# Softmax sums and turned maxima share one PSUM bank behind the V products; a maximum over partitions by matmul; two small re-orderings

## The chip, the core and the metric

The kernel runs on one core of a Trainium2 chip. That core has five engines with a queue each: TensorE (PE; its weight loads are listed as PEld), VectorE (DVE), ScalarE (ACT), GpSimd (POOL) and SyncE (SP, which here only issues DMAs). The metric is device time in microseconds (us); lower is better. Before the change it is 2773.54 us, the median of three runs (2772.81 to 2776.64).

## The reference: what is computed

One bidirectional encoder layer is applied to two requests of 2048 tokens and 1024 features with the same weights:

```python
u = rmsnorm(h);  q, k, v, ga, f, gf = split(u @ w_in)     # 512,128,128,512,512,512 columns
q, k = rope(rmsnorm(q)), rope(rmsnorm(k))                 # 8 query heads, 2 key/value heads of 64
a  = softmax(q k^T / 8) v * silu(ga)
fo = Re(fft2 over positions and 64 channels of f) @ w_fmix * silu(gf)
h  = h + concat(a, fo) @ w_out
h  = h + (p @ w_ple) * sigmoid(rmsnorm(h) @ w_ple_gate)
y  = rmsnorm(h)
```

All data are float32 and large gains make the softmax sharp, so the kernel splits the matrix operands into a high and a low half-precision part (three products for each matmul) and subtracts the exact row maximum ahead of the exponential.

## The kernel before, in words

**Stages.** Three stages follow one another. From 0 to about 845 us the projections (line L444) run and their results go to DRAM. From there to about 2697 us attention runs, and while it runs a second stream of work, the *filler*, is cut into its steps: first the Fourier branch (`fourier2`, L1010 to L1072), then the output projection, the gate and the norms (`outp`, L1445). What is left of the filler when attention ends is the *tail*.

**Attention.** A unit `u` is a block of 128 queries of one request and one key/value head with four query heads; there are `n` = 64 units with eight steps `j` = 0 to 7 each, one for every 256 keys. A step `g = 8u + j` issues, in this order: deferred work (`flush`), the scores of step j (`scores`, L1137, then two exponentials on ACT, L1140, and an addition of the exponentials on POOL, L1143/L1145), one eighth of the row maxima of a later unit (`maxima`: two matmuls at L1164 into the tile `ps_m`, one reduction on DVE at L1172), and at j = 4 and j = 0 the products of four steps with V (`pv`, L1202). A step with such products is called heavy. `ps_m` has one buffer, so the maxima matmuls of a step can begin only when DVE has done the reduction of the step before.

**Row sums.** At j = 4 of unit u, ahead of the products with V, `sums(u-1)` multiplies the added exponentials by ones (L1236) into a bank, and DVE takes the reciprocal (L1238) and scales the result (L1239).

**Turned maxima.** At j = 4 ACT writes the negated maxima of unit u+1 to `nm` (L1182); at j = 6 `max_rows(u+1)` turns them with an identity matmul (L1188) into another bank, and DVE writes `mr` from it (L1190). The first scores of unit u+1 read `mr`.

**The banks.** Both take a PSUM bank from `bank()`. In the first part of the filler that is one of three (`ps_f`, `ps_g` twice); once `outp` has begun (`self.grouped`) it is always the single buffer `ps_f`, which the filler's embedding product (L444, `ps_f<-wp,pT`, released by DVE at L1405 and L1407) uses too.

**Order and pace.** During attention PE, ACT, DVE and SP run in the order in which the program is written (`manual_schedule`); POOL is ordered by a planner with a cost model. `interleave` hands the filler a budget after each step, `FILL` = 775 us of the program's own accounting in all; a heavy step yields a share of 0, so nothing is normally filled in behind it. In the tail the planner orders all engines.

**The scale of the output projection.** `mix(s)` needs a maximum over 128 partitions of three per-partition maxima: `mix_max` reduces on DVE and calls `partition_all_reduce` on POOL (L1310), `mix_scale` works on the result (L1316 and after). It runs twice, once for each request.

**Loads and stores touched.** `fourier2` loads `bd` (L1734, 512 KB, in `fill`) and `c2x` (L1037) ahead of the first `c` (L979) and `g_in` (L984), all on SP. `project` collects the stores of transposed q and k in `stores_next` (L739, L743) and issues them at the start of the next iteration:

```python
            stores, stores_next = stores_next, []
            for f in stores:
                f()
            ...
            if i == n + 3:
                self.drain(bg)
                self.drain(self.ahead)
                for f in stores_next:
                    f()
```

`lo_q(i - 3)`, which fills that list, runs for the last time in iteration n + 2. The DRAM store of a unit's result (`agd<-at`, L1242) is issued on SP in the step after `sums`. In `slot`, a small copy `seen` (L1422) on DVE makes the second half of a grouped projection wait for the first.

Of the kernel before, what the change touches and what calls it, by code (L numbers as in the profile page):

```python
# [10 lines left out]
F32 = mybir.dt.float32  # L11
# [3 lines left out]
ALU = mybir.AluOpType  # L15
AX = mybir.AxisListType
PSUM = bass.MemoryType.PSUM
# [10 lines left out]
K_ONE = 2.0 ** 12  # L28

CAP = 5.0  # L30
FILL = 775.0
AHEAD = 13
PVG = 4
NBF = 5
# [10 lines left out]
_E = mybir.EngineType  # L45
# [94 lines left out]
class Build:  # L140
    def __init__(self, ctx, tc, a, y):
        self.ctx, self.tc, self.nc = ctx, tc, tc.nc
        self.a, self.y = a, y
        nc = self.nc
        ep = ctx.enter_context
        self.const = ep(tc.tile_pool(name="const", bufs=1))
        self.st = ep(tc.tile_pool(name="st", bufs=2))
        self.psF = ep(tc.tile_pool(name="psF", bufs=1, space=PSUM))
        self.psG = ep(tc.tile_pool(name="psG", bufs=2, space=PSUM))
        self.grouped = False  # L150
# [408 lines left out]
    def project(self, P, PU, W, early, wkv, wq, wga, bg, mid):  # L559
# [3 lines left out]
        nc, st = self.nc, self.st  # L563
# [159 lines left out]
        def lo_q(i):  # L723
            s, c = steps[i]
            t1 = T1.pop(i)
            qs, ks = QS.pop(i)
            res = KD.pop(i)
            kv = lambda b: ks[:, :, b].rearrange("p v t d -> p t v d")
            KS[i] = P.tile([128, CH, 2, 64], F32, name="ksum", bufs=1)
            nc.vector.tensor_tensor(out=res[:], in0=res[:], in1=kv(1), op=ALU.subtract)  # L730
            nc.vector.tensor_copy(kv(2), res[:])
            nc.vector.tensor_tensor(out=res[:], in0=res[:], in1=kv(2), op=ALU.subtract)
            nc.vector.tensor_tensor(out=KS[i][:], in0=t1[:, :, 8:10, :], in1=res[:], op=ALU.subtract)
            nc.vector.tensor_tensor(out=qs[:, :, :, 1, :], in0=t1[:, :, 0:8, :], in1=qs[:, :, :, 0, :], op=ALU.subtract)
            for tt in range(CH):
                t = c * CH + tt
                qT = P.tile([128, 8, 128], F16, name="qT", bufs=2)
                nc.sync.dma_start_transpose(qT[:], qs[:, tt].rearrange("p h b d -> p (h b d)"))
                stores_next.append(lambda t=t, qT=qT: nc.sync.dma_start(self.qTd[s][t], qT[:]))  # L739
            kT = P.tile([128, 2, 3, 128], F16, name="kT", bufs=1)  # L740
            nc.sync.dma_start_transpose(kT[:].rearrange("p v y r -> p (v y) r"),
                                        ks[:].rearrange("p v y t d -> p (v y t d)"))
            stores_next.append(lambda: nc.sync.dma_start(self.kTd[s][:, :, c].rearrange("v p y r -> p v y r"), kT[:]))  # L743

        def sweep_part(us):

# [31 lines left out]
        def iteration(i):  # L778
# [180 lines left out]
    def fourier2(self, pool, hook):  # L959
# [135 lines left out]
    def attention(self, kvp):  # L1095
# [89 lines left out]
        def max_rows(u):  # L1185

            ps = self.bank()
            nc.tensor.matmul(ps[:, 0:128], nm[:], self.ident[:], start=True, stop=True)  # L1188
            MR[u] = mr = kvp.tile([128, 4, 128], F16, name="mr", bufs=1)
            nc.vector.tensor_tensor(out=mr[:], in0=ps[:, 0:128].unsqueeze(1).to_broadcast([128, 4, 128]),  # L1190
                                    in1=own[:].unsqueeze(2).to_broadcast([128, 4, 128]), op=ALU.mult)

        def pv(u, j0):
# [32 lines left out]

            self.defer(lambda: self.defer(add))

        def sums(u):

            s, kv, t = units[u]
            acc, at = ACC.pop(u), AT.pop(u)
            av = acc[:, 0, :].rearrange("p (c e q) -> p e c q", e=2, q=128)
            ps = self.bank()
            for e in range(2):
                nc.tensor.matmul(ps[64 * e:64 * e + 64, 0:256], ones[:], av[:, e], start=True, stop=True)  # L1236
            r, x = ps[:, 256:512], at[:].rearrange("p c q -> p (c q)")
            nc.vector.reciprocal(r, ps[:, 0:256])  # L1238
            nc.vector.tensor_tensor(out=x, in0=x, in1=r, op=ALU.mult)  # L1239
# [23 lines left out]
            if k == 1 and 0 <= v - 1 < n:  # L1263
                negate(v - 1)

        def turn(g):
            v, k = divmod(g + 2, 8)
            if k == 0 and 0 <= v < n:
                max_rows(v)
# [9 lines left out]
        ones = pool.tile([128, 64], F32, name="ones", bufs=1)  # L1279
        nc.gpsimd.memset(ones[:], 1.0)  # L1280
        fresh = {last[0, kv]: kv for kv in range(2)}
        for g in range(8 * n + 7):
            self.step = g
            self.flush()
            u, j = g // 8, g % 8
            if j == 0 and 0 <= u and u + 2 < n:
                load_q(u + 2)
            if j == 4 and u - 1 in fresh:
                load_kv(1, fresh[u - 1])
            if 0 <= u < n:  # L1290
                scores(u, j)
            self.drain(lead(g))
# [6 lines left out]
            turn(g)  # L1299
            yield 0 if heavy else RATE if g >= 8 * n // 2 else 1 if g > FIRST else SLOW  # L1300


    def mix_max(self, s):
        nc, st = self.nc, self.st
        m = st.tile([128, 4], F32, name="mx4")
# [4 lines left out]
        nc.gpsimd.partition_all_reduce(mm[:, 0:3], m[:, 0:3], 128, bass_isa.ReduceOp.max)  # L1310
        return mm

    def mix_scale(self, s, mm):
        nc, st = self.nc, self.st
# [7 lines left out]

    def mix(self, s, out):

        sc = []
        yield from self.after(self.defer(lambda: sc.append(self.mix_max(s))), 1)
        yield from self.after(self.defer(lambda: out.append(self.mix_scale(s, sc[0]))))

    def outp(self, pool0, ow, open_pool):

# [305 lines left out]
    def run(self):  # L1636
# [91 lines left out]

        def fill():
            self.nw2k = NW  # L1730
            C0 = fill_stack.enter_context(pool("C0", side="right"))
            with pool("B", side="right") as B:
                self.bd = B.tile([128, 2, 4, 128], F32, name="bd")
                nc.sync.dma_start(self.bd[:], self.bdd)  # L1734
                ow = {}

                def wload(n, k, pool):
# [90 lines left out]
```

## Time and profile before

| | |
|---|---|
| median of three runs | 2773.54 us |
| the profiled execution: its own time | 2775.26 us |
| its span (first to last instruction) | 2773.5 us |
| mean granted TensorE clock | 0.989 |
| busy share PE / DVE / ACT / POOL | 96 / 61 / 44 / 59 % |
| DMA, mean over the span | 107 GB/s |

The profile comes from one execution whose own time is 1.72 us above the median and 1.76 us above its span. A group line names the source line, engine, operation and tiles, then the count, the busy time and the mean duration in ns, and last the idle time ahead of it and what ended that. In a timeline a row gives start, length, engine and line; square brackets hold the idle time of that engine just before. "issue" means that the engine was idle with no visible cause. Ends of matmuls are modelled, so two rows on PE overlap a little; starts are the better measure.

### The profile page before, as it was taken

Reading aid. Unit: us, or ns where it says so; the run is one execution under the profiler, and the core shown is the slowest. Engines: PE = TensorE matmul, PEld = TensorE weight load, DVE = VectorE, ACT = ScalarE, POOL = GpSimd, SP = SyncE. Lnnn points to the kernel's source line nnn. Section 1 sums busy time; section 2 is a strip of 40 time slices with the busy share of each in tenths; the row PEclk is TensorE's granted clock in tenths of the full one; section 3 lists DMA queues with packets and bytes.
Section 4 is the critical chain, followed back from the end, with each engine's and each line's share of the span. In section 5 each row is a group of like instructions: output and inputs, shape, how many; then the busy total and the mean of one; then the engine's idle time right before and its main releaser. Section 6 shows DMA issues by size and latency. Waiting matters only on the chain.

```text
span 2773.5 us, 46318 instructions
## 1 busy us (share of the span) xinstructions
PE 2656.9 (96%) x18236; PEld 1264.5 (46%) x18236; DVE 1684.4 (61%) x2469; ACT 1214.7 (44%) x2047; POOL 1636.9 (59%) x1394
## 2 busy tenths in 40 slices
PE   6899999999998989999999999999999999999998
PEld 3455565655555543443444434433443344434433
DVE  6755555564564664666666766666656666666644
ACT  3443333432224543554445554444444445444541
POOL 1233224332336786777768877776677677767760
PEclk9999999999999999999999999999999999999998
DMA  7467566674428752222222223322222232222222
GB/s 231 143 192 187 175 184 180 185 179 121 129 70 238 236 169 88 56 71 54 69 56 54 69 67 82 82 62 71 56 67 60 60 82 54 67 71 64 63 73 61
DMA packets 418555, 296.74 MB, mean 107 GB/s; under 512 B 259456, under 2 KB 360000, under 8 KB 418336
## 3 DMA queue, kind: packets, MB, share of 16 engines
q1 hardware_dynamic: 405424, 252.01, 34.7%
q0 software_dynamic: 12912, 41.77, 4.2%
q8 instruction: 143, 2.34, 0.3%
q14 instruction: 76, 0.62, 0.1%
HBM read 149.50 MB, written 86.51 MB: 85 GB/s over the span
## 4 chain that ended last, share of the span: by engine, by line
PE 83%; DVE 7%; issue 3%; DMA 2%; POOL 2%; ACT 2%; SPq 0%; DVEq 0%; POOLq 0%; ACTq 0%
PE ps_g L1445 22%; PE ps_o L1202 15%; PE ps_x L444 14%; PE ps_s L1137 12%; PE ps_f L444 6%; PE ps_g L444 6%; PE ps_m L1164 3%; DVE a_mx L1172 1%; PE ps_f L1236 1%; PE ps_f L1188 1%; ACT p L1140 1%; POOL acc L1145 1%; PE ps_g L1056 1%; DVE h L1407 1%; DVE ps_f L1405 1%
## 5 line engine op out<-in xcount | busy, mean ns | idle before, releaser
L1145 POOL TENSOR_TENSOR acc<-acc,p 128x1024 f32<-128x1024 f32 x384 | 917.2, 2388 | 225.4 <-ACT p L1140 163.2
L1140 ACT ACTIVATE p<-ps_s,s_scale 128x512 f32<-128x512 f32 x1024 | 648.0, 684 | 692.9 <-PE ps_s L1137 667.4
L1172 DVE TENSOR_REDUCE a_mx<-ps_m 128x1 f32<-128x1024 f32 x499 | 610.4, 1223 | 534.6 <-PE ps_m L1164 525.6
L1445 PE MATMUL ps_g<-w_pg,hT 64*128 64x512 f16 x2832 | 507.8, 378 | 5.4 <-DVE seen L1422 3.0
L1202 PE MATMUL ps_o<-p,v 128*64 128x512 f32 x2048 | 467.0, 598 | 0.0
L1137 PE MATMUL ps_s<-q,k 64*128 64x512 f16 x3072 | 438.7, 378 | 7.6 <-ACT p L1140 7.4
L444 PEld LDWEIGHTS <-uc 128*128 128x128 f16 x3072 | 301.6, 98 | 311.3 <-issue 22.1
L1445 PEld LDWEIGHTS <-hT 64*128 64x128 f16 x2832 | 206.2, 94 | 169.4 <-issue 19.7
L1445 PE MATMUL ps_g<-w_wo,mh 64*128 64x512 f16 x1488 | 269.6, 378 | 3.6 <-DVE mh L1367 2.3
L1137 PEld LDWEIGHTS <-k 64*128 64x128 f16 x3072 | 148.8, 94 | 261.2 <-issue 140.5
L1445 PE MATMUL ps_g<-w_wo,mT 64*128 64x512 f16 x1488 | 264.5, 376 | 0.4 <-DMA mT<-mh 0.3
L1202 PEld LDWEIGHTS ps_o<-p,v 128*64 128x64 f32 x2048 | 143.8, 137 | 255.7 <-issue 247.2
L1164 PE MATMUL ps_m<-k,q 64*128 64x512 f16 x998 | 205.1, 377 | 16.6 <-DVE a_mx L1172 15.7
L1143 POOL TENSOR_TENSOR acc<-p,p 128x1024 f32<-128x1024 f32 x64 | 150.5, 2352 | 98.2 <-ACT p L1140 97.9
L444 PEld LDWEIGHTS <-w_ga 128*128 128x128 f16 x1536 | 151.5, 99 | 53.1 <-issue 22.6
L926 POOL DMA_DIRECT2D gfd<-gt x32 | 19.3, 602 | 218.1 <-DVE gt L954 213.2
L1445 PEld LDWEIGHTS <-mh 64*128 64x128 f16 x1488 | 101.7, 94 | 97.9 <-issue 17.4
L1445 PEld LDWEIGHTS <-mT 64*128 64x128 f16 x1488 | 107.2, 94 | 81.2 <-DMA mT<-mh 1.3
L1218 ACT ACTIVATE tb<-ps_o,a_scale 64x256 f32<-64x256 f32 x128 | 60.1, 469 | 164.2 <-PE ps_o L1202 163.4
L444 PE MATMUL ps_x<-uc,w_ga 128*128 128x256 f16 x1008 | 115.0, 275 | 5.1 <-ACT ge L911 4.5
L944 POOL DMA_DIRECT2D agd<-gat x64 | 35.9, 561 | 134.1 <-DVE gat L954 134.0
L1238 DVE RECIPROCAL ps_f<-ps_f 128x256 f32<-128x256 f32 x60 | 105.4, 1756 | 7.6 <-PE ps_f L1236 7.6
(317 smaller groups left out, 3365.7 us busy)
## 6 DMA issues: line engine op xcount, KB each, us to landing
q<-qTd SPq DMA_DIRECT2D x256, 64.0 KB, 2.3
ag<-agd SPq DMA_DIRECT2D x64, 256.0 KB, 3.2
out<-h POOLq DMA_DIRECT2D x31, 512.0 KB, 3.2
x<-in_x_prompt SPq DMA_DIRECT2D x16, 512.0 KB, 4.8
w_st<-in_w_out SPq DMA_DIRECT2D x32, 256.0 KB, 4.1
gfd<-gt POOLq DMA_DIRECT2D x32, 256.0 KB, 3.4
gd<-ge POOLq DMA_DIRECT2D x32, 256.0 KB, 3.7
agd<-gat POOLq DMA_DIRECT2D x64, 128.0 KB, 2.4
```

The costliest lines, as they stand in the source:

```text
L444: self.nc.tensor.matmul(ps, lhs(ia, k), rhs(ib, k), start=(i == 0), stop=(i == 3 * ks - 1))
L944: nc.gpsimd.dma_start(self.agd[s][1, r * 128:(r + 1) * 128, c * n:(c + 1) * n], gt[:, :n])
L1137: nc.tensor.matmul(S[u][e][:], w[sl], q[sl].rearrange("p h q -> p (h q)"), start=j == i == 0, stop=i + 1 == len(todo), skip_group_check=True)
L1140: nc.scalar.activation(p[:, e, :], S[u][e][:], AF.Exp, scale=self.sc["s_scale"][:])
L1143: nc.gpsimd.tensor_tensor(out=ACC[u][:], in0=P[u, 0][:], in1=p[:], op=ALU.add)
L1145: nc.gpsimd.tensor_tensor(out=ACC[u][:], in0=ACC[u][:], in1=p[:], op=ALU.add)
L1164: nc.tensor.matmul(ps[c], Q[u][0][sl, h, :], kt[s, kv, half][sl, :, 0, :], start=True, stop=True)
L1172: nc.vector.reduce_max(MX[u][:, h, half, c:c + 1], x, axis=AX.X)
L1202: nc.tensor.matmul(o[64 * e:64 * e + 64, :], vt[s, kv, c // 8][:, c % 8, :], p[:, e, :], start=(j == 0), stop=(j == 7))
L1218: nc.scalar.activation(tb[64 * e:64 * e + 64], ov[64 - 64 * e:128 - 64 * e, e], AF.Copy, scale=self.sc["a_scale"][64 - 64 * e:128 - 64 * e ...
L1238: nc.vector.reciprocal(r, ps[:, 0:256])
L1445: nc.tensor.matmul(g[0][:], g[1](ia, k)[sl], g[2](ib, k)[sl], start=a, stop=z, skip_group_check=True)
```

## The change

Six edits come together.

1. At j = 4, `sums(u-1)` and `max_rows(u+1)` run behind `pv` and write two parts of one bank; then DVE makes `mr`, then the reciprocal in place, then the scaling (`divide`). `max_rows` moves from j = 6 to j = 4.
2. `mix` makes the maximum over partitions with an identity matmul, a reduction on DVE and a matmul with ones, in place of `partition_all_reduce`.
3. `c2x` and `bd` are loaded behind the first `c` and `g_in`.
4. `self.last_stores` is set to GpSimd's queue at i == n + 3.
5. The tail runs with PE in program order.
6. `FILL` is 781 in place of 775.

```diff
-FILL = 775.0
+FILL = 781.0
...
+        self.grouped, self.last_stores = False, nc.sync
...
-                stores_next.append(lambda t=t, qT=qT: nc.sync.dma_start(self.qTd[s][t], qT[:]))
+                stores_next.append(lambda t=t, qT=qT: self.last_stores.dma_start(self.qTd[s][t], qT[:]))
...
             if i == n + 3:
                 self.drain(bg)
                 self.drain(self.ahead)
+                self.last_stores = nc.gpsimd
                 for f in stores_next:
                     f()
...
         cx = pool.tile([128, 128], F32, name="c2x", bufs=1)
-        nc.sync.dma_start(cx[:], self.a["c_dft2x"])
         for t in range(FP):
             loads(t)
-        while todo:
-            todo.pop(0)()
+            while todo:
+                todo.pop(0)()
+            if t == 0:
+                nc.sync.dma_start(cx[:], self.a["c_dft2x"])
+                nc.sync.dma_start(self.bd[:], self.bdd)
...
+        def divide(u, r):
...
+            nc.vector.reciprocal(r, r)
             nc.vector.tensor_tensor(out=x, in0=x, in1=r, op=ALU.mult)
...
             self.drain(lead(g))
-            if j == 4 and 0 <= u - 1 < n:
-                sums(u - 1)
             heavy = (g - 1) % PVG == PVG - 1 and 0 <= g - 1 < 8 * n
             if heavy:
                 self.run_slow(2 if j == 0 else 1)
                 pv((g - 1) // 8, (g - 1) % 8 - PVG + 1)
-            turn(g)
+            if j == 4:
+                ps = self.bank()
+                if u > 0:
+                    sums(u - 1, ps[:, 0:256])
+                if u + 1 < n:
+                    max_rows(u + 1, ps[:, 256:384])
+                if u > 0:
+                    divide(u - 1, ps[:, 0:256])
             yield 0 if heavy else RATE if g >= 8 * n // 2 else 1 if g > FIRST else SLOW
...
-        mm = st.tile([128, 4], F32, name="mx4r")
-        nc.gpsimd.partition_all_reduce(mm[:, 0:3], m[:, 0:3], 128, bass_isa.ReduceOp.max)
...
+        m = self.small.tile([128, 64], F32, name="mx4", bufs=1)
+        nc.gpsimd.memset(m[:], 0.0)
+        yield from self.after(self.defer(lambda: self.mix_max(s, m)))
+        ps = self.bank()
+        nc.tensor.matmul(ps[0:64, 0:128], m[:], self.ident[:], start=True, stop=True)
+        r, mm = [st.tile([128, 4], F32, name=f"mx4{b}", bufs=1) for b in "rs"]
+        nc.vector.memset(r[:], 0.0)
+        nc.vector.tensor_reduce(out=r[0:64, 0:1], in_=ps[0:64, 0:128], op=ALU.max, axis=AX.X)
+        nc.vector.tensor_scalar(out=m[:], in0=self.ident[:, 0:64], scalar1=r[:, 0:1], scalar2=None, op0=ALU.mult)
+        yield from self.after([self.nflush])
+        ps = self.bank()
+        for e in range(2):
+            nc.tensor.matmul(ps[64 * e:64 * e + 64, 0:64], self.ones[:], m[:], start=True, stop=True)
+        nc.vector.tensor_copy(mm[:, 0:3], ps[:, 0:3])
+        yield None
+        yield from self.after(self.defer(lambda: out.append(self.mix_scale(s, mm))))
...
-                nc.sync.dma_start(self.bd[:], self.bdd)
...
-        with pool("psD", 5, space=PSUM) as self.psX:
+        with pool("psD", 5, space=PSUM) as self.psX, tc.manual_schedule(engines={_E.PE}):
             self.drain(f)
```

More of the change, by code (lines that the diff above doesn't have):

```diff
@@ L149, in __init__ @@
         self.psG = ep(tc.tile_pool(name="psG", bufs=2, space=PSUM))
-        self.grouped = False
+        self.grouped, self.last_stores = False, nc.sync
         self.psX, self.nx = None, 0
@@ L742, in lo_q @@
                                         ks[:].rearrange("p v y t d -> p (v y t d)"))
-            stores_next.append(lambda: nc.sync.dma_start(self.kTd[s][:, :, c].rearrange("v p y r -> p v y r"), kT[:]))
+            stores_next.append(lambda: self.last_stores.dma_start(self.kTd[s][:, :, c].rearrange("v p y r -> p v y r"), kT[:]))
         def sweep_part(us):
@@ L1183, in negate, with max_rows @@
                                  m[:].unsqueeze(1).to_broadcast([128, 2, 4]), AF.Copy, scale=-1.0 / K_ONE)
-        def max_rows(u):
-            ps = self.bank()
-            nc.tensor.matmul(ps[:, 0:128], nm[:], self.ident[:], start=True, stop=True)
+        def max_rows(u, ps):
+            nc.tensor.matmul(ps, nm[:], self.ident[:], start=True, stop=True)
             MR[u] = mr = kvp.tile([128, 4, 128], F16, name="mr", bufs=1)
-            nc.vector.tensor_tensor(out=mr[:], in0=ps[:, 0:128].unsqueeze(1).to_broadcast([128, 4, 128]),
+            nc.vector.tensor_tensor(out=mr[:], in0=ps.unsqueeze(1).to_broadcast([128, 4, 128]),
                                     in1=own[:].unsqueeze(2).to_broadcast([128, 4, 128]), op=ALU.mult)
@@ L1227, in gather, with sums @@
             self.defer(lambda: self.defer(add))
-        def sums(u):
-            s, kv, t = units[u]
[L1232 to L1238, printed above, removed]
+        def sums(u, ps):
+            acc = ACC.pop(u)
+            av = acc[:, 0, :].rearrange("p (c e q) -> p e c q", e=2, q=128)
+            for e in range(2):
+                nc.tensor.matmul(ps[64 * e:64 * e + 64], self.ones[:], av[:, e], start=True, stop=True)
+        def divide(u, r):
+            s, kv, t = units[u]
+            at = AT.pop(u)
+            x = at[:].rearrange("p c q -> p (c q)")
+            nc.vector.reciprocal(r, r)
             nc.vector.tensor_tensor(out=x, in0=x, in1=r, op=ALU.mult)
@@ L1264, in lead @@
                 negate(v - 1)
[L1266 to L1269, printed above, removed]
         def leads():
@@ L1274, in leads @@
                 yield
-                turn(g)
+                if g == -2:
+                    max_rows(0, self.bank()[:, 0:128])
         self.ahead = leads()
         pool = yield 0.0
-        ones = pool.tile([128, 64], F32, name="ones", bufs=1)
-        nc.gpsimd.memset(ones[:], 1.0)
+        self.ones = pool.tile([128, 64], F32, name="ones", bufs=1)
+        nc.gpsimd.memset(self.ones[:], 1.0)
         fresh = {last[0, kv]: kv for kv in range(2)}
@@ L1298, in attention, with mix_max @@
                 pv((g - 1) // 8, (g - 1) % 8 - PVG + 1)
-            turn(g)
+            if j == 4:
[6 more added lines that the diff above has]
+                    divide(u - 1, ps[:, 0:256])
             yield 0 if heavy else RATE if g >= 8 * n // 2 else 1 if g > FIRST else SLOW
-    def mix_max(self, s):
-        nc, st = self.nc, self.st
-        m = st.tile([128, 4], F32, name="mx4")
+    def mix_max(self, s, m):
+        nc = self.nc
         nc.vector.tensor_reduce(out=m[:, 0:1], in_=self.tmax[s][:], op=ALU.max, axis=AX.X)
@@ L1308, in mix_max @@
         nc.vector.tensor_reduce(out=m[:, 2:3], in_=self.fmax[s][:], op=ALU.max, axis=AX.X)
-        mm = st.tile([128, 4], F32, name="mx4r")
-        nc.gpsimd.partition_all_reduce(mm[:, 0:3], m[:, 0:3], 128, bass_isa.ReduceOp.max)
-        return mm
     def mix_scale(self, s, mm):
@@ L1323, in mix @@
     def mix(self, s, out):
-        sc = []
-        yield from self.after(self.defer(lambda: sc.append(self.mix_max(s))), 1)
-        yield from self.after(self.defer(lambda: out.append(self.mix_scale(s, sc[0]))))
+        nc, st = self.nc, self.st
+        m = self.small.tile([128, 64], F32, name="mx4", bufs=1)
[9 more added lines that the diff above has]
+        ps = self.bank()
+        for e in range(2):
+            nc.tensor.matmul(ps[64 * e:64 * e + 64, 0:64], self.ones[:], m[:], start=True, stop=True)
+        nc.vector.tensor_copy(mm[:, 0:3], ps[:, 0:3])
+        yield None
+        yield from self.after(self.defer(lambda: out.append(self.mix_scale(s, mm))))
     def outp(self, pool0, ow, open_pool):
@@ L1730, in fill @@
             self.nw2k = NW
-            C0 = fill_stack.enter_context(pool("C0", side="right"))
+            self.small = C0 = fill_stack.enter_context(pool("C0", side="right"))
             with pool("B", side="right") as B:
                 self.bd = B.tile([128, 2, 4, 128], F32, name="bd")
-                nc.sync.dma_start(self.bd[:], self.bdd)
                 ow = {}
```

## The prediction

> **What bounds the kernel now.** I read the page first, then the waits of PE, then timelines of PE, DVE, POOL and SP around each edit, and the clock by stage. PE is the bound nearly everywhere:
>
> ```profile
> PE 2656.9 (96%) x18236; PEld 1264.5 (46%) x18236; DVE 1684.4 (61%) x2469; ACT 1214.7 (44%) x2047; POOL 1636.9 (59%) x1394
> ```
>
> So a change pays only through PE: by less time between matmul starts, or by waits of PE that go. These are the waits that the edits touch (who waited for whom: total us, times, longest):
>
> ```profile
> PE ps_m L1164 <- DVE a_mx L1172: 15.7, 15, 5.6
> ...
> PE ps_f L1236 <- DVE h L1407: 6.2, 8, 0.8
> PE ps_f L444 <- DVE mr L1190: 6.0, 4, 1.5
> PE ps_f L1188 <- DVE h L1407: 5.8, 9, 0.7
> PE ps_g L1056 <- DMA g_in<-gd: 5.2, 1, 5.2
> ...
> PE ps_g L1445 <- DVE seen L1422: 4.3, 2, 3.0
> ```
>
> The three ps_f rows are the single bank of the grouped phase: sums and turned maxima find the embedding's bank not yet released (6.2 + 5.8), and an embedding finds `mr` not yet written (6.0).
>
> **Edit 1, what it takes away on PE.** One ordinary unit, from the sums at j = 4 to the turned maxima at j = 6:
>
> ```profile
> 1664.19 0.65 PE L1236 MATMUL ps_f<-acc,ones 128*64 128x256 f32 x4 [0.77 <-DVE h L1407]
> 1664.64 3.63 PE L1202 MATMUL ps_o<-p,v 128*64 128x512 f32 x16
> 1668.21 0.82 PE L1137 MATMUL ps_s<-q,k 64*128 64x512 f16 x6
> 1668.86 0.38 PE L1164 MATMUL ps_m<-k,q 64*128 64x512 f16 x2
> 1669.08 2.11 PE L1445 MATMUL ps_g<-w_wo,mh 64*128 64x512 f16 x18
> ...
> 1671.67 0.38 PE L1164 MATMUL ps_m<-k,q 64*128 64x512 f16 x2
> 1671.98 0.49 PE L1188 MATMUL ps_f<-ident,nm 128*128 128x128 f32 x2
> 1672.40 0.82 PE L1445 MATMUL ps_g<-w_wo,mh 64*128 64x512 f16 x6
> ```
>
> By starts, the sums take 0.45 us (1664.19 to 1664.64). The turned maxima take 0.51: from the maxima to the next filler matmul it is 0.73 with them (1671.67 to 1672.40) and 0.22 without (1668.86 to 1669.08). Of that, 0.09 is the change from half precision to float32 (0.31 against 0.22 behind the maxima). Together 0.96 us a unit. Behind `pv`, which is float32 too, sums and turned maxima cost 0.45 + 0.42. The trace has no such joints. If they are free, and the change back to half precision is paid once where `pv` and the turned maxima paid it separately (again 0.09), the unit is 0.18 us shorter; if both new joints cost 0.09, it is as long as before. The nearest row, sums to `pv`, shows no extra, so I take 0.15: over 61 units **-9 us** (bounds -11 and 0).
>
> The bank waits go as well. Sums now come 3.6 us later, when the embedding's bank is long free, and one allocation replaces two: 6.2 + 5.8 + 6.0 = **-18 us**.
>
> **Edit 1, what it adds.** The cover of the DVE work was `pv`: reciprocal and scaling ran while PE did 3.57 us of products. Now they and `mr` start when `pv` is over, and DVE keeps program order, so the maxima reduction of j = 5 stands behind all three, and the maxima matmuls of j = 6 need `ps_m` from that reduction. A heavy step is followed by no filler that could cover it. The trace holds this order once, by accident, when DVE was late behind a POOL operation:
>
> ```profile
> 1449.34 1.76 DVE L1238 RECIPROCAL ps_f<-ps_f 128x256 f32<-128x256 f32 x1
> 1451.13 0.42 DVE L1239 TENSOR_TENSOR at<-at,ps_f 128x256 f32<-128x256 f32 x1
> 1451.47 1.22 DVE L1172 TENSOR_REDUCE a_mx<-ps_m 128x1 f32<-128x1024 f32 x1
> ```
> ```profile
> 1452.74 0.39 PE L1164 MATMUL ps_m<-k,q 64*128 64x512 f16 x2 [0.28 <-DVE a_mx L1172]
> ```
> ```profile
> L1190 DVE TENSOR_TENSOR mr<-ps_f,own 128x512 f16<-128x512 f32 x60 | 40.8, 681 | 4.6 <-PE ps_f L1188 4.6
> ```
>
> The reciprocal began at 1449.34 and PE got `ps_m` at 1452.74: 3.40 us. Call T the start of the scores of j = 5. The turned maxima end 0.07 us after the following matmul starts (1671.98 + 0.49 against 1672.40), so `mr` starts near T + 0.1, takes 0.68, and `ps_m` is free at about T + 0.12 + 0.60 + 3.40 = **T + 4.1** (the reciprocal overlaps the end of `mr` by 0.08, as the reduction does that of the scaling above). In the unit above PE wants it at 1671.67 - 1668.21 = T + 3.46. How much filler lies between differs, and the units fall into classes:
>
> ```profile
> 1148.30 0.82 PE L1137 MATMUL ps_s<-q,k 64*128 64x512 f16 x6
> ...
> 1151.76 0.38 PE L1164 MATMUL ps_m<-k,q 64*128 64x512 f16 x2
> ```
> ```profile
> 2623.48 0.82 PE L1137 MATMUL ps_s<-q,k 64*128 64x512 f16 x6
> ...
> 2626.94 0.38 PE L1164 MATMUL ps_m<-k,q 64*128 64x512 f16 x2
> ```
> ```profile
> 1058.19 0.82 PE L1137 MATMUL ps_s<-q,k 64*128 64x512 f16 x6
> ...
> 1061.01 0.43 PE L1164 MATMUL ps_m<-k,q 64*128 64x512 f16 x2
> ```
> ```profile
> 2596.15 0.82 PE L1137 MATMUL ps_s<-q,k 64*128 64x512 f16 x6
> ...
> 2598.97 0.44 PE L1164 MATMUL ps_m<-k,q 64*128 64x512 f16 x2
> ```
> ```profile
> 1776.94 0.82 PE L1137 MATMUL ps_s<-q,k 64*128 64x512 f16 x6
> 1777.60 0.38 PE L1164 MATMUL ps_m<-k,q 64*128 64x512 f16 x2
> 1777.91 1.47 PE L444 MATMUL ps_f<-wp,pT 128*128 128x512 f16 x6
> ```
>
> Of 61 units, 21 are of the 3.46 class (first and last shown first), each short by 0.65: 14 us. Eleven are of the 2.8 class (first and last shown next), short by 1.25: 14 us. In 14 the filler is long enough, and five lie in the Fourier part. In the others the bank comes first: an embedding wants `ps_f` at T + 0.97 (1776.94 to 1777.91), while the scaling ends only at T + 2.9. That is 2.0 us in six units, 0.7 in four where a chunk of filler precedes it, and by estimate 3 in all in the Fourier part, where three banks turn: 18 us. Edit 1 thus adds **+46 us**. The low bound is 18 (were every unit's cover like that of the long ones, with the bank's waits left), the high one 51 (a slot of the projection that starts in j = 6 would wait for L1383, 0.45 us, in ten units by estimate). Behind the waiting scaling on SP stands the store of the unit's result, and behind that the filler's loads and transposes of j = 5, up to 3 us later than now; their users are steps away.
>
> **Edit 2.** POOL stops around the all-reduce, before it and after it:
>
> ```profile
> 968.95 0.38 POOL L1310 PARTITION_ALL_REDUCE mx4r<-mx  x1 [5.99 <-issue]
> 977.51 2.35 POOL L1145 TENSOR_TENSOR acc<-acc,p 128x1024 f32<-128x1024 f32 x1 [8.18 <-issue]
> ```
> ```profile
> 986.52 0.61 PE L1164 MATMUL ps_m<-k,q 64*128 64x512 f16 x2 [5.58 <-DVE a_mx L1172]
> ```
> ```profile
> 985.00:995.00 10.00, 8.48 (x32) 2.74 (x32) 4.92 (x6) 0.29 (x1) 9.92 (x6) 0.66 0.54 169
> ```
>
> That is 14.5 us of POOL. Its backlog held the Fourier products that DVE was to reduce, DVE held `ps_m`, and PE waited 5.58 us; the granted clock was then 0.66 over ten microseconds, 3.4 us lost. So 9.0 us go in the first use; the second (0.28 us above) cost little. The new chain adds three small float32 matmuls with their two changes of precision, about 0.5 us each time, and DVE waits for PE and PE for DVE at the single bank, say as long as the 0.77 above: 1.3 us twice. Net **-7 us** (bounds -10, and -2 if POOL, busy there anyway, is late without it too).
>
> The Trainium skill (GPSIMD Engine Reference, Instruction dispatch) says that the first call of a freshly loaded kernel pays an instruction load of about 6 us. The 5.99 agrees; the 8.18 behind it is not in that rule, and by the rule alone POOL would be back 8 us sooner and little of the 5.58 would be the all-reduce's, which would leave this edit near +2 and the sum 9 us higher.
>
> **Edit 3.** SP issues in order:
>
> ```profile
> 853.96 0.39 SPq L1734 DMA_DIRECT2D bd<-bdd  x1
> ...
> 855.52 0.80 SPq L984 DMA_DIRECT2D g_in<-gd  x2
> ```
>
> The first `g_in` is issued 0.96 us earlier, and 576 KB no longer go ahead of it, so the 5.2 us wait loses 1 to 3 us: **-2 us** (bounds -4 with some half-clock time, -1). `bd` is next needed some 5 us later and comes in time.
>
> **Edit 4** does nothing: as written, the list is empty when the new queue is set, for `lo_q` last ran an iteration earlier and its stores were issued on SP ahead of that line. 0 us.
>
> **Edits 5 and 6.** The tail stalls once, because DVE takes `mh` ahead of `seen`:
>
> ```profile
> 2709.16 1.28 DVE L1367 SCALAR_TENSOR_TENSOR mh<-ag,mix_s,mh 128x1024 f16<-128x1024 f32 x1 [7.55 <-ACT mh L1362]
> 2710.36 0.15 DVE L1422 COPY seen<-ps_g 128x1 f32<-128x1 f32 x1
> ```
> ```profile
> 2712.00:2724.00 12.00, 12.00 (x34) 4.15 (x32) 6.06 (x18) 2.24 (x4) 0.71 (x2) 0.57 0.50 94
> ```
>
> PE waits 3.0 us, and the clock of 0.57 over the next twelve costs 5.2 more. Only PE is put in program order; DVE, which makes the stall, stays with the planner. If the order turns round, 8 us go; if it stays, PE loses the matmuls that were hoisted over the wait, about 1.5 us. Moving 6 us of filler ahead of the end shifts work without removing any. I take **-4 us** (bounds -8 and +2).
>
> The Trainium skill (TensorE: Matmul & The Clock Gate, HAM clock gate) lets the clock fall to half after an idle window of 3.4 us. Here a wait of 3.0 us was enough, so the trace puts the limit lower. By the rule a stall cut to well under the window costs no clock and a longer one the same again, so this edit would come out at an end, -8 or +2, and not between.
>
> **Sum.** -9 - 18 + 46 - 7 - 2 - 4 = **+6 us** on the profiled span of 2773.5. That execution's own time is 2775.26, 1.72 above the median of the runs; the sum moves both alike, so for the median I forecast 2773.54 + 6 = 2780.
>
> **Rivals.** *The burst is mostly covered (faster).* The burst decides, and its cover is the filler behind j = 5. If the changed emission puts another chunk there (0.65 us more), the 3.46 class waits for nothing, the 2.8 class keeps 0.6 (7 us) and the bank's waits keep some 13 of 18: 46 becomes 20, the sum -20, 2754. For it: DVE is 61% busy and has slack overall. Against it: the accident of 1449, where this order did stop PE even with 4.3 us of cover.
>
> *The tail's stall and its half clock go altogether (about even).* Then -4 becomes -8, and with the new joints free -9 becomes -11: the sum is 0, 2774. For it: PE had waited 1.5 us when L1367 started (the wait ended with `seen` at 2710.5, 3.0 us long), so `seen` could have run first. Against it: DVE's order is not in the edit.
>
> *The backlog spreads (clearly slower).* DVE is late at j = 5 in each unit; at the high bounds (+51, joints 0, tail +2) the sum is +26, 2800. It decides if L1383 and the loads behind the store are late too.
>
> **Chances.** A measurement here can tell about 0.2%, 5.5 us, from no change. Forecast 0.45 (own range 2770 to 2790: faster 0.03, same 0.16, slower 0.26); burst covered 0.28 (faster); tail 0.12 (faster 0.04, same 0.08); backlog 0.15 (slower). Faster 0.35, same 0.24, slower 0.41. The range 2752 to 2798 leaves out a little of the second case and of the last.
>
> **What would show it.** Right: PE's wait at ps_m on a_mx grows from 15.7 us to some 35, and ps_f on L444 waits for `at` (L1239), some 15 us; the waits of L1236 and L1188 for L1407 are gone; no 8.18 on POOL; the wait for `g_in` is between 2 and 4; the last qTd and kTd stores still on SP. Wrong: if ps_m's wait stays under 15 us, the burst is covered and the time is near 2754.

## The result, and the profile after

The changed kernel takes 2819.72 us (median of 4 runs, 2819.05 to 2823.96), the kernel before on the same chip 2775.09: a ratio of 1.016, interval 1.014 to 1.018, that is 44.6 us slower. The forecast was 2780 in a range of 2752 to 2798. The profiled execution has a span of 2822.2, 48.7 more than before.

The waits of PE in the changed kernel (who waited for whom: total us, times, longest), to be laid beside those of before in the prediction:

```profile
PE ps_m L1167 <- DVE a_mx L1175: 41.4, 50, 2.5
...
PE ps_s L1140 <- ACT p L1143: 16.5, 45, 0.8
PE ps_f L444 <- DVE at L1244: 9.9, 6, 2.1
...
PE ps_g L1462 <- DMA hT<-h_hl: 6.3, 4, 3.4
...
PE ps_g L444 <- ACT th L1413: 4.7, 1, 4.7
PE ps_g L1462 <- DVE h L1400: 4.4, 12, 0.9
PE ps_g L1059 <- DMA g_in<-gd: 3.0, 1, 3.0
```

Three rows of the kernel before that the prediction does not show:

```profile
PE ps_s L1137 <- ACT p L1140: 8.9, 27, 0.7
...
PE ps_g L1445 <- DVE mh L1367: 2.3, 4, 0.8
PE ps_g L1445 <- DMA hT<-h_hl: 2.2, 1, 2.2
```

The three rows of the single bank (6.2, 6.0 and 5.8) are gone. The wait of the maxima grew from 15.7 to 41.4, and a new one for the scaled result `at` stands at 9.9. Both kinds were forecast, at some 35 and some 15. Not forecast are the 7.6 us more for the exponentials, the 4.1 more for hT, and the 4.67 for `th`, which lies in the tail.

One ordinary unit around j = 5, PE first and then DVE (start, duration, engine and line, then in brackets the idle time before and who ended it):

```profile
1682.53 3.65 PE L1204 MATMUL ps_o<-p,v 128*64 128x512 f32 x16
1686.01 0.60 PE L1236 MATMUL ps_f<-acc,ones 128*64 128x256 f32 x4
1686.54 0.49 PE L1190 MATMUL ps_f<-ident,nm 128*128 128x128 f32 x2
1686.96 0.82 PE L1140 MATMUL ps_s<-q,k 64*128 64x512 f16 x6
...
1691.20 0.39 PE L1167 MATMUL ps_m<-k,q 64*128 64x512 f16 x2 [0.61 <-DVE a_mx L1175]
```
```profile
1687.07 0.69 DVE L1192 TENSOR_TENSOR mr<-ps_f,own 128x512 f16<-128x512 f32 x1 [3.21 <-PE ps_f L1190]
1687.79 1.77 DVE L1243 RECIPROCAL ps_f<-ps_f 128x256 f32<-128x256 f32 x1
1689.59 0.42 DVE L1244 TENSOR_TENSOR at<-at,ps_f 128x256 f32<-128x256 f32 x1
1689.93 1.22 DVE L1175 TENSOR_REDUCE a_mx<-ps_m 128x1 f32<-128x1024 f32 x1
```

The joints behind the products are nearly as cheap as assumed: 0.53 us for the sums (0.45 was taken), 0.42 for the turned maxima, and then scores at once. DVE, idle for 3.21 us while PE was at the products, then does four things in a row, and PE gets `ps_m` at 1691.20. With T = 1686.96, the start of the scores of j = 5, that is T + 4.24 (forecast T + 4.1).

The next lines show a place in the second half of the attention that no step of the prediction speaks of. Scores follow maxima directly, three steps in a row, and each time they wait for the exponentials:

```profile
2111.64 0.38 PE L1167 MATMUL ps_m<-k,q 64*128 64x512 f16 x2
2112.82 0.37 PE L1140 MATMUL ps_s<-q,k 64*128 64x512 f16 x1 [0.79 <-ACT p L1143]
...
2113.84 0.57 PE L1167 MATMUL ps_m<-k,q 64*128 64x512 f16 x2
2115.01 0.37 PE L1140 MATMUL ps_s<-q,k 64*128 64x512 f16 x1 [0.59 <-ACT p L1143]
...
2116.03 0.57 PE L1167 MATMUL ps_m<-k,q 64*128 64x512 f16 x2
2117.03 0.37 PE L1140 MATMUL ps_s<-q,k 64*128 64x512 f16 x1 [0.42 <-ACT p L1143]
```

No filler was issued between them. Counted in the trace between 1110 and 2660 us, this happens 4 times before and 15 times after. It is the mark by which the filler's rate is followed below ("steps without filler").

Where the time went can be worked out from the starts of matmuls. From the 17th group of products with V to the 125th the kernel before needs 1530.8 us, the changed one 1574.4, so 43.6 more. For each kind of neighbours on PE (groups of the same length) I take the time from start to start above the shortest one seen in either kernel, and add it up:

| group, and what it follows | before | after | change |
|---|---|---|---|
| maxima behind scores | 10.8 | 47.4 | +36.6 |
| embedding behind maxima or filler | 1.7 | 11.7 | +10.0 |
| scores behind maxima | 2.3 | 11.8 | +9.5 |
| filler and products behind maxima | 5.9 | 13.9 | +8.0 |
| sums and turned maxima behind maxima | 16.5 | none | -16.5 |

The shortest times themselves sum to 4.4 less, though 5.2 us more of filler is among them; smaller kinds make the rest of the 43.6.

### The profile page after: what moved, and what is told of

Same layout as the page of the kernel before. It is cut to its first block, busy times and chain, and to the rows that moved or that the text cites. A ratio compares the mean times of both kernels' runs of the same rounds, so it can differ in the third digit from the quotient of the medians.

```text
span 2822.2 us, 46402 instructions
## 1 busy us (share of the span) xinstructions
PE 2676.4 (95%) x18272; PEld 1276.1 (45%) x18272; DVE 1698.2 (60%) x2463; ACT 1213.4 (43%) x2047; POOL 1647.1 (58%) x1411
## 4 chain that ended last, share of the span: by engine, by line
PE 81%; DVE 11%; DMA 3%; ACT 2%; issue 2%; SPq 1%; POOL 1%; DVEq 0%; ACTq 0%; POOLq 0%
PE ps_g L1462 20%; PE ps_x L444 16%; PE ps_o L1204 15%; PE ps_s L1140 10%; PE ps_f L444 7%; PE ps_g L444 6%; PE ps_m L1167 3%; DVE ps_f L1243 2%; DVE a_mx L1175 2%; ACT p L1143 1%; DVE mr L1192 1%; PE ps_f L1236 1%; PE ps_f L1190 1%; DMA gf_in<-gfd 1%; DVE h_hl L1516 1%
## 5 line engine op out<-in xcount | busy, mean ns | idle before, releaser
L1462 PEld LDWEIGHTS <-hT 64*128 64x128 f16 x2880 | 214.7, 94 | 170.4 <-issue 20.0
L1204 PEld LDWEIGHTS ps_o<-p,v 128*64 128x64 f32 x2048 | 136.5, 137 | 275.8 <-issue 275.4
L1167 PE MATMUL ps_m<-k,q 64*128 64x512 f16 x998 | 206.0, 379 | 42.3 <-DVE a_mx L1175 41.4
L1462 PEld LDWEIGHTS <-mh 64*128 64x128 f16 x1488 | 104.4, 94 | 94.4 <-issue 15.7
L1167 PEld LDWEIGHTS <-q 64*128 64x128 f16 x1024 | 64.9, 94 | 123.7 <-issue 68.8
L1192 DVE TENSOR_TENSOR mr<-ps_f,own 128x512 f16<-128x512 f32 x58 | 40.1, 691 | 128.8 <-PE ps_f L1190 128.8
```

Source lines behind the costliest of these rows:

```text
L1167: nc.tensor.matmul(ps[c], Q[u][0][sl, h, :], kt[s, kv, half][sl, :, 0, :], start=True, stop=True)
L1192: nc.vector.tensor_tensor(out=mr[:], in0=ps.unsqueeze(1).to_broadcast([128, 4, 128]), in1=own[:].unsqueeze(2).to_broadcast([128, 4, 128]), ...
L1204: nc.tensor.matmul(o[64 * e:64 * e + 64, :], vt[s, kv, c // 8][:, c % 8, :], p[:, e, :], start=(j == 0), stop=(j == 7))
L1462: nc.tensor.matmul(g[0][:], g[1](ia, k)[sl], g[2](ib, k)[sl], start=a, stop=z, skip_group_check=True)
```

## The experiments

Each ratio is against the kernel before, run on the same chip in the same series; us are worked out from it on 2777.

**1. Edit 1 undone, all else changed.**

```diff
+            if j == 4 and u > 0:
+                ps = self.bank()
+                sums(u - 1, ps[:, 0:256])
+                divide(u - 1, ps[:, 0:256])
...
                 pv((g - 1) // 8, (g - 1) % 8 - PVG + 1)
-            if j == 4:
...
+            if j == 6 and u + 1 < n:
+                max_rows(u + 1, self.bank()[:, 0:128])
```

> Edit 1 is taken back (sums and division ahead of the products with V, turned maxima at j = 6 in a bank of their own); all other edits stay. Theory (the division behind the products sits on VectorE in front of the maxima reduction, and that is most of the loss): the waits of the maxima matmuls on the reduction fall from 41.4 us to under 12, and the time falls by 33 to 48 us, to 2772 to 2787. Rival (a third or more of the loss is made by the other edits, the filler's rate and the tail's order): it falls by 15 to 30 us only, to 2790 to 2805, and the score matmuls still wait some 16 us for the exponentials.

Measured 1.0058 (1.0042 to 1.0074), +16 us. The waits on the reduction fell to 8.9 us, but that on the exponentials stayed at 17.5, with 15 steps without filler. The rival held: at this FILL a good third of the loss is not edit 1's.

**2. Only the division back ahead of the products.**

The same edit, but the turned maxima stay at j = 4:

```diff
+            if j == 4 and u + 1 < n:
+                max_rows(u + 1, self.bank()[:, 0:128])
```

> Only the sums and the division go back ahead of the products with V; the turned maxima stay behind them at j = 4, now in a bank of their own. VectorE then has only the 0.68 us of mr in front of the reduction of j = 5. Theory (reciprocal and scaling are the burst): the shortest time from the scores of j = 5 to the maxima of j = 6 falls from 4.24 us back to the 2.8 and 3.46 of before, the ps_m waits fall under 12 us, the time falls by 30 to 45 us, to 2775 to 2790. Rival (the early mr and the joint bank do the harm): the waits stay above 25 us and the time stays above 2805.

Measured 1.0019 (1.0009 to 1.0030), +5 us.

```profile
PE ps_m L1167 <- DVE a_mx L1175: 7.8, 14, 2.1
```

The shortest time from the scores of j = 5 to the maxima of j = 6 is back at 2.82 and 3.46 us in the two classes of the prediction. The theory held: of the changed kernel's 44.6 us the place of the division makes some 39. And it beats experiment 1, where the turned maxima stand at j = 6 again, by 11 us: the early `mr` is the useful half of edit 1.

**3. The tail left to the planner, all else changed** (`tc.manual_schedule(engines={_E.PE})` of the tail taken out).

> The changed kernel without the written-out order of TensorE in the tail (FILL stays 781). Theory (program order in the tail lost the hoisted matmuls and brought the 4.67 us wait at 2755.6 with 17 us at half clock): 6 to 10 us faster than the changed kernel, 2810 to 2814. Rival (the planner would make the same stalls with less filler left): within 3 us of the changed kernel, 2817 to 2822.

Measured 1.0161 (1.0142 to 1.0181), not to be told from the changed kernel (1.016). The rival held.

**4. FILL 781 alone on the kernel before.**

> The kernel before with FILL 781 in place of 775, nothing else. Theory (the higher rate lets the filler run out of results to work on, so that scores follow maxima with nothing between and wait for the exponentials, the 7.6 us more of that wait): 4 to 12 us slower than before, 2779 to 2787. Rival (6 us of filler are only moved ahead of the end): within 3 us of before.

Measured 1.0112 (1.0097 to 1.0128), **+31 us**: theory and rival both missed, the theory in size. Its waits of PE:

```profile
PE ps_s L1137 <- ACT p L1140: 20.6, 54, 2.0
...
PE ps_g L1445 <- DVE mh L1367: 7.4, 10, 1.5
...
PE ps_g L1445 <- DMA hT<-h_hl: 6.0, 4, 1.7
...
PE ps_x L444 <- ACT mh L1362: 4.1, 1, 4.1
PE ps_g L1445 <- DMA mT<-mh: 3.3, 4, 1.1
```

Before, these were 8.9, 2.3, 2.2, none and 0.3. There are 15 steps without filler, the same steps by number as in the changed kernel, and behind them the filler comes five times in a lump of 36 or 48 matmuls (once before), whose own chain (`mh`, hT, mT) is then in the open. The next lines follow one tile of the filler through one such place, from the store of the attention unit that it needs to its products:

```profile
2087.03 0.38 SPq L1242 DMA_DIRECT2D agd<-at  x1
2088.92 0.37 SPq L1344 DMA_DIRECT2D ag<-agd  x1
```
```profile
2104.38 1.15 ACT L1362 ACTIVATE mh<-ag,mix_s 128x1024 f16<-128x1024 f32 x1
```
```profile
2113.08 2.21 DVE L1367 SCALAR_TENSOR_TENSOR mh<-ag,mix_s,mh 128x1024 f16<-128x1024 f32 x1
```
```profile
2115.35 0.39 PE L1445 MATMUL ps_g<-w_wo,mh 64*128 64x512 f16 x1 [1.02 <-DVE mh L1367]
```

The tile is loaded 1.9 us behind the store, and its operand `mh` is made from it by 2115.3. PE has no filler from 2097.4 to 2113.7, and three steps without filler lie in that stretch. So the filler has caught up with the attention: it has used up its products before the next tile is ready. The short distance from store to load alone does not tell this, for it is as short (2.2 us or less) in 24 of the 32 tiles of the kernel before. In the program the filler waits in these two lines, where `pr` loads the next tile and makes `mh`; at each `None` that they yield, `interleave` ends the filling of the step:

```python
                yield from pr
                yield from self.after(tm.pop())
```

By starts, as in the table above, the stretch from the 17th to the 125th products is 33.2 us longer than before. Scores behind maxima take 9.5 of it, scores behind filler 8.8, maxima behind scores 5.3, and 8.6 are filler that now runs here. In exchange the tail is 5.1 us shorter.

**5. The changed kernel with FILL 775.**

> The changed kernel with FILL back at 775; every other edit stays. Theory (the 31 us that FILL 781 alone costs add to the rest): 2784 to 2794 beside a kernel before of 2775, and the steps in which scores follow maxima with nothing between fall from 15 back to about 4. Rival (the filler runs dry only because other edits move with it, and edit 1 carries the loss by itself): 2805 or more.

Measured 1.0091 (1.0073 to 1.0108), +25 us, between theory and rival. The steps without filler are 4 again, as the theory has it, but only 19 of the 31 us go.

```profile
PE ps_m L1167 <- DVE a_mx L1175: 40.6, 50, 1.7
...
PE ps_f L444 <- DVE at L1244: 15.8, 10, 2.2
```

**6. Division ahead of the products, turned maxima behind, FILL 775.**

> Division ahead of the products with V, turned maxima behind them at j = 4, and FILL 775: edits 2 to 5 and the useful half of edit 1. Theory (both causes of the loss are gone, the bank's waits of j = 6 and the all-reduce too): 16 to 28 us faster than the kernel before. Rival (the two causes overlap, since a filler that is held up by VectorE also falls behind less): within 6 us of before.

Measured 0.9938 (0.9924 to 0.9952), **-17 us**: the theory held, at its near end.

**7. Edits 2 and 3 alone.**

> Edits 2 and 3 alone on the kernel before (the maximum over partitions by TensorE, g_in's order), with the old order of sums, FILL 775 and the planner's tail. Forecast of the prediction: -7 and -2, so 9 us faster, 5 to 13. Rival (GpSimd is late there without the all-reduce too): within 3 us.

Measured 0.9955 (0.9942 to 0.9968), **-12 us**. Two of its waits, and the stretch in which the all-reduce stood before (length, busy us of PE, PEld, DVE, ACT and POOL, then granted clock, DMA share, GB/s):

```profile
PE ps_m L1167 <- DVE a_mx L1175: 8.1, 12, 1.3
...
PE ps_g L1059 <- DMA g_in<-gd: 2.6, 1, 2.6
```
```profile
960.00:1000.00 40.00, 40.00 (x290) 23.60 (x288) 29.91 (x43) 24.14 (x41) 35.56 (x23) 1.00 0.83 259
```

PE is busy throughout at full clock. The forecast held.

**8. The written-out tail alone, FILL 775.**

> The kernel before with TensorE in program order in the tail, FILL 775. Forecast of the prediction: -4 us, from -8 (the stall of 2.96 us and its half clock go) to +2 (the stall stays and the hoisted matmuls are lost). The run with the planner's tail showed no difference under FILL 781, which speaks for a value within 3 us of nothing.

Measured 1.0010 (1.0001 to 1.0018), +3 us. DVE's order in the tail is the old one and the stall is longer (4.2 us in place of 3.0):

```profile
2713.16 1.28 DVE L1367 SCALAR_TENSOR_TENSOR mh<-ag,mix_s,mh 128x1024 f16<-128x1024 f32 x1 [8.22 <-ACT mh L1362]
2714.36 0.15 DVE L1422 COPY seen<-ps_g 128x1 f32<-128x1 f32 x1
```
```profile
PE ps_g L1445 <- DVE seen L1422: 5.6, 2, 4.2
```

**9. A short reciprocal in the changed kernel, FILL 775.**

```
-            nc.vector.reciprocal(r, r)
+            nc.vector.reciprocal(r[:, 0:64], r[:, 0:64])
```

This kernel leaves out the reciprocal of 192 of the 256 columns, so its output is not the layer's; only the length of this one instruction is changed.

> The changed kernel with FILL 775, in which the reciprocal takes 64 of its 256 columns and leaves the rest as they are (three quarters of the results are then multiplied by the sum instead of its inverse): about 0.5 us instead of 1.76, in the same place and order. Theory (the length of the work in front of the reduction is what PE waits for): the shortest time from the scores of j = 5 to the maxima of j = 6 falls from 4.24 to about 3.0 us, the ps_m waits from 40.6 to under 15 us, the waits of the embedding for the scaled result from 15.8 to about 5, and the time falls by 28 to 38 us against FILL 775 with the full reciprocal, to 10 us faster than the kernel before or better. Rival (the joints behind the products and the order of the waits cost, not the length): less than 12 us of it go.

Measured 0.9893 (0.9880 to 0.9907), -30 us, and 55 us less than experiment 5, more than the 28 to 38 expected. The reciprocal's rows in the changed kernel and here (count, shortest/median/longest in ns):

```profile
L1243 DVE RECIPROCAL ps_f<-ps_f x59: 1766/1767/1767, 1056.9 to 2747.3; 128x256 f32<-128x256 f32 x59
```
```profile
L1243 DVE RECIPROCAL ps_f<-ps_f x60: 566/566/567, 1015.4 to 2666.5; 128x64 f32<-128x64 f32 x60
```
```profile
PE ps_m L1167 <- DVE a_mx L1175: 5.9, 11, 1.2
...
PE ps_f L444 <- DVE at L1244: 5.5, 6, 1.0
```

1.2 us less on DVE in 64 places take 34.7 us off the wait for the maxima and 10.3 off that for `at`, and nothing was moved. The shortest time from the scores of j = 5 to the maxima of j = 6 falls from 4.24 to 3.04 us. So the length of the work in front of the reduction is the cause, not the place of the sums on PE. What the expectation left out follows from those waits: 6.8 us were lost to half clock between the 17th and the 125th products in experiment 5 and none here, and the filler's wait for L1400 falls from 4.1 to 1.0.

**10 and 11. Division ahead, turned maxima behind, the planner's tail; FILL 775 and FILL 769.**

> Division ahead of the products, turned maxima behind them, FILL 775, and the tail left to the planner. Theory (the tail's program order alone costs 2 to 3 us): 18 to 22 us faster than the kernel before, ratio about 0.993. Rival (the tail's order makes no difference here): as with the written-out tail, about 17 us.

> As the run beside it, with FILL 769. Theory (781 costs because the filler overtakes the attention; below that point a lower rate only moves filler into the tail, which is on the path too): no more than 4 steps without filler, the last products with V some 6 us earlier, the end within 4 us of FILL 775. Rival (775 is a lucky setting and any other rate upsets the order): 10 us or more slower than FILL 775, with more waits ahead of the tail.

Measured 0.9934 (0.9920 to 0.9947), not to be told from experiment 6; and 0.9877 (0.9864 to 0.9890), 2742.73 us, **34 us faster than the kernel before**. At 769 no step is without filler. But both guesses on 769 missed: the last products come 19.6 us earlier than in experiment 10, not 6, and the tail takes only some 6 of that back.

**12. Division behind the products, turned maxima at j = 6, FILL 775.**

> FILL 775, sums and division behind the products with V as in the changed kernel, but the turned maxima back at j = 6 in a bank of their own. VectorE has then 2.2 us in front of the reduction of j = 5 instead of 2.9, and PE gets to it 0.4 us sooner. Theory (each part of the burst counts by its length): shortest time from the scores of j = 5 to the maxima of j = 6 about 3.2 us, ps_m waits 15 to 22 us, time 2 to 14 us slower than the kernel before. Rival (the division behind the products costs its full amount whatever follows it): as the changed kernel with FILL 775, about 25 us slower.

Measured 1.0012 (1.0003 to 1.0021), +3 us, as the theory has it. This rests on the time alone: no row of its profile is used, so the shortest time and the waits of the expectation are not shown.

**13 to 16. The rate.** FILL 769 and 787 on the kernel before; 763 and 757 beside the early division and the planner's tail.

> The kernel before with FILL 769, nothing else. Theory (the filler overtakes the attention at 781 and in part at 775): the 4 steps without filler go, 8 to 18 us faster than before. Rival (775 fits the old order, and any other rate unsettles it): slower than before by 5 us or more. In between: within 4 us, if 769 gains only beside the early division.

> The kernel before with FILL 787. Theory (overtaking): more than the 15 steps without filler of FILL 781, and 35 to 60 us slower than before. Rival (781 is an accident of rounding): 20 us or less slower.

> Early division, mr behind the products, planner's tail, FILL 763. Theory (with no step left without filler, 6 us less filler are only moved into the tail): within 5 us of FILL 769, 0.986 to 0.990 of the kernel before. Rival (each 6 us of filler taken out of the attention save 12 to 30 us, as from 781 to 775 to 769): 0.984 or less.

> As the run beside it, FILL 757. Theory: the tail grows by what the attention loses, within 6 us of FILL 769, and nearer to it or above it than FILL 763. Rival: 0.980 or less of the kernel before.

| FILL | kernel before | steps without filler | early division | steps without filler |
|---|---|---|---|---|
| 757 | | | 0.9889 (0.9876 to 0.9903) | 0 |
| 763 | | | 0.9902 (0.9889 to 0.9916) | 0 |
| 769 | 0.9964 (0.9950 to 0.9978) | 0 | 0.9877 (0.9864 to 0.9890) | 0 |
| 775 | 1 | 4 | 0.9934 (0.9920 to 0.9947) | 4 |
| 781 | 1.0112 (1.0097 to 1.0128) | 15 | 1.0019 (1.0009 to 1.0030), written-out tail | 15 |
| 787 | 1.0208 (1.0194 to 1.0222) | 27 | | |

The theories on 769, 787 and 757 held; 763 came 7 us above 769 where 5 were allowed. The time rises with the steps without filler, in the old order by 10, 31 and 27 us from one FILL to the next, and beside the early division it stops falling where there are none. With FILL 787 the wait for the exponentials is longest of all:

```profile
PE ps_s L1137 <- ACT p L1140: 29.4, 74, 1.9
```

The rival that 775 merely fits the old order is out: 769 is faster. That 763 is 0.25% above 769 stays unexplained.

## Why the prediction was wrong, point by point

From the runs, on 2777: edits 2 and 3 together give -12 and the written-out tail +3, both measured on the kernel before. Edit 1 at FILL 775 is +35 (experiment 5 less these two), and FILL 781 on top of these is +19 (the changed kernel less experiment 5). The last two are differences, so the four close to the 44.6 measured by construction. The prediction had -9 for edits 2 and 3, +19 for edit 1, and -4 for tail and FILL together. So tail and FILL are off by 26 us, edit 1 by 16.

**The step that failed: edit 6.** "Moving 6 us of filler ahead of the end shifts work without removing any" took FILL for a quantity of work. The shift itself is there: with FILL 781 the tail of the kernel before is 5.1 us shorter. But FILL is a rate as well. It sets how close the filler runs behind the attention that feeds it, and at 775 it already touched it 4 times. At 781 there are 15 steps in which the filler has used up its products before the next tile is ready; there the scores have no cover and wait for the exponentials, and the filler's own chain comes into the open. Alone it costs 31 us, in the changed kernel 19. Both show the same 15 steps. By the tables of waits, those for `mh` and mT grow by 8.1 us in the old order, while the changed kernel has none of them, and its wait for `at` falls from 15.8 to 9.9; together that is about the difference of 12. Why `mh` and mT are in time there stays open.

**Edit 1, the burst: mechanism right, the term for the maxima too small.** T + 4.1 measured T + 4.24, so the two classes were short by 0.78 and 1.42 instead of 0.65 and 1.25. And more units waited than the 32 counted: the profile has 50 waits in experiment 5. The units with 24 matmuls of filler (4.11 us of cover), held to be covered, come out at 4.24, and those of the Fourier part (3.61), for which only the bank was priced, at 4.31. Against experiment 7, which lacks edit 1, the maxima behind scores cost 33.5 us more by starts from the 17th to the 125th products and some 10 more ahead of them, where the prediction had 28. The embedding's waits (13.2 us more behind maxima, 3.0 behind filler) are near the 18. The wait for L1400 (L1383 before) came as its bound said (4.1 us in 12 waits). The loss of clock was in no term: experiment 5 loses 8.5 us more to half clock during the attention than experiment 7.

**Edit 1, what it takes away: right, one part smaller.** The bank's rows (18 us) are gone. By the rows shown, sums, products and turned maxima took 4.02 + 0.51 us in a unit before and take 4.43 now (1682.53 to 1686.96), so a unit is 0.10 us shorter, where 0.15 was taken: some 6 us in place of 9.

**Edits 2 and 3: right, -12 for -9, inside the bounds of -14 and -3; the two were not measured apart.** The 8.18 us on POOL are gone; in the changed kernel POOL goes on at once behind the memset of the new chain:

```profile
971.31 0.15 POOL L1330 MEMSET mx<- 128x64 f32 x1
971.45 1.27 POOL L1150 TENSOR_TENSOR acc<-acc 128x512 f32<-128x512 f32 x1
```

The rival reading by the Trainium skill (GPSIMD Engine Reference, Instruction dispatch), by which most of the 5.58 us wait would have stayed and this edit come out near +2, is not borne out: the gap behind the call went with the call as well. In the kernel before, the second call stands between gaps too, 5.79 us before it and 6.89 behind it, so the stop is not one of the first call alone.

**Edit 4: right.** The last qTd and kTd stores are still issued on SP, ahead of `g_in`, which now goes ahead of `bd`:

```profile
846.65 2.78 SPq L739 DMA_DIRECT2D qTd<-qT  x2
849.96 0.37 SPq L743 DMA_DIRECT2D kTd<-kT  x1
...
853.63 0.80 SPq L985 DMA_DIRECT2D g_in<-gd  x2
...
854.96 0.42 SPq L1044 DMA_DIRECT2D bd<-bdd  x1
```

**Edit 5: the far end of its bounds.** The order on DVE stayed, as the prediction feared, and the stall with it: +3 alone, where the bound was +2 and the value taken -4. In experiments 3 and 10 the tail's order makes no difference that can be told from nothing. With FILL 781 the tail has another hole, and its half clock (the second block's columns as in experiment 7):

```profile
2760.26 2.72 PE L444 MATMUL ps_g<-wp,pT 128*128 128x512 f16 x6 [4.67 <-ACT th L1413]
```
```profile
2754.00:2778.00 24.00, 19.33 (x62) 6.63 (x58) 6.76 (x8) 3.94 (x5) 4.57 (x11) 0.64 0.30 75
```

**The rivals.** The burst was not covered. "The backlog spreads" had the sign and ended 20 us short, at 2800: it counted waits of the kind of L1383, not the filler's rate. No case held the true one.

## What to carry to other kernels

A constant that paces background work can be a rate with a cliff. Look for steps in which the background had nothing to issue, and if the profile shows even a few, try a lower rate first: here the 4 steps at 775 went at 769, for 10 us. Before a group of instructions is moved from ahead of a long PE block to behind it, add up what each other engine then does in one piece, and check it against the shortest cover among all units, not the ordinary one. An edit with several parts is measured part by part: here two gave 12 us, half of edit 1 gave some 6 more (0.9934 in experiment 10 against 0.9955, whose intervals just overlap), and the rest took it all back.

## What the runs showed of the hardware

A wait of 2.07 us can cost PE its clock. Two such waits in the changed kernel, then the stretch around the second (columns as in experiment 7):

```profile
1126.16 1.47 PE L444 MATMUL ps_f<-wp,pT 128*128 128x512 f16 x6 [2.07 <-DVE at L1244]
...
1660.07 2.74 PE L444 MATMUL ps_f<-wp,pT 128*128 128x512 f16 x6 [2.07 <-DVE at L1244]
```
```profile
1658.00:1664.00 6.00, 3.93 (x16) 1.25 (x18) 4.17 (x5) 1.15 (x3) 4.21 (x2) 0.72 0.36 109
```

The same six matmuls took 2.74 us at 1660.07, where the granted clock was 0.72 over six microseconds, and 1.47 behind a wait as long at 1126.16. In experiment 5 four of six waits of 2.07 to 2.16 us were followed by 3.41 us at half clock, 1.7 us lost each, so a wait of 2 us can cost 3.7. The Trainium skill (TensorE: Matmul & The Clock Gate, HAM clock gate) has a free-running window of 3.4 us and lets the clock fall after an idle one. That the same wait costs clock at one time and not at another agrees with a free-running window; that a whole idle window is needed does not agree with waits of 2.07 us.

A reciprocal on DVE is long for its size: 1767 ns for 256 columns and 566 for 64, so 6.3 ns for each further column. The maxima reduction above takes 1.22 us for 1024 columns, 1.2 ns a column.
